# Expert stage of a hybrid block: every 64-token block in fp32, the first in straight code, further ones nested behind one branch

## The chip, the cores and the metric

The kernel runs on one core of one Trainium2 chip. The metric is the device time of one execution in microseconds (us), as the median of several runs. PE is the matrix engine (PEld its weight loads, PEq its sequencer), DVE the vector engine, ACT the scalar engine, POOL the GpSimd engine, and SP the engine that only issues transfers here.

## The reference, cut to what matters

The block computes an adaLN-modulated sub-layer of pooling heads and Mamba-2 heads with one output projection, then a mixture of experts, then a final RMSNorm. Only the expert part bears on the change:

```python
# 1024 tokens, D = 1024, 32 experts, two experts per token
# h: normed tokens; counts[e]: tokens of expert e (data dependent)
hu = h[rows_of_e] @ w13[e]                 # 1024 -> 2 x 512, fp32
a, b = split(hu)
y = (silu(a) * b) @ w2[e]                  # 512 -> 1024, fp32
out[rows_of_e] += g2 * gate * y
```

With the fixed inputs the 32 experts hold 2 to 397 tokens. In blocks of 64 tokens, 23 experts are one block, six are two (experts 8, 12, 17, 20, 26, 30), two are three (21, 22) and expert 16 is seven: 48 blocks.

## The kernel before, in words

Everything up to the routing is straight code. The expert stage then runs through the 32 experts in a Python loop, so each has its own instructions. The token counts are only known on the chip: each engine loads an expert's count into a register (`values_load`, L1194) and branches on it.

Weights. An expert needs twelve transfers of 512 KB (eight chunks of `w13`, four of `w2`). SP issues them in expert order (`load_to`, L793), at most `Q` = 4 in flight, into a ring of 39 slots; the ring's slots are tiles that earlier stages have given up (`raw`, `ybf`, `yps`, `wo`, `xc`, `g1b`, `h`, `x`, `sc`, `sh`), which is why the weight operands of one and the same matmul have many names in the rows. 36 transfers are issued ahead of the stage. Refills stand at the end of each expert: eight inside the branch (`refill()`), four behind the down projection.

Tokens. POOL gathers a block of token rows (`fetch`, L1067); PE transposes it (`transposed`, four matmuls named `px`, L1073), ACT copies it to `xa`. The results are weighed on DVE (L1145) and added to `acc` in memory by POOL's scatter (L1160).

Branches. `If(rv > 64, label e{e})` (L1264) has the code for more than 64 tokens as its fall-through, and the code for up to 64 tokens in its `Else`, so an expert of one block jumps.
- Up to 64 tokens: `up64` does the up projection in fp32, 64 matmul records on `xa`; `gated` (L1093, L1094) applies SiLU and the product; `turned` transposes the result (L1132) and, between its two halves, the next expert's tokens.
- More than 64: ACT and DVE split tokens and the eight `w13` chunks into fp16 high and low parts (L57, L59), and PE does three fp16 passes over 128 tokens (`up128s`); inside stands `If(rv > 128, label b{e})` (L1282), and below it `more` with branches L1221 and L1235 for still more tokens.
- Behind the If, for every expert: a hint, the down projection of the first 64 tokens (32 matmul records), the last four refills.

Hints. `aim(name)` puts a branch hint ("likely taken") for the named branch into every engine's instructions. `aim("e{e+1}")` stands ahead of the down projection of expert e, so on PE 32 matmul records ahead of the branch; `aim("b{e}")` stands first behind the fall-through of L1264.

Of the kernel before, what the change touches and what calls it, by code (L numbers as in the profile page):

```python
# [8 lines left out]
F32 = mybir.dt.float32  # L9
# [10 lines left out]
NT = 8  # L20
# [13 lines left out]
EARLY = 2  # L34
# [10 lines left out]
def block_kernel(ctx: ExitStack, tc: tile.TileContext, x, c, w_ada, b_ada, w_in, w_pool, pool_scale,  # L45
# [742 lines left out]
    lds = []  # L788

    def load_to(n):  # L790
        for i in range(loaded[0], min(n, 12 * NE)):
            e, k = divmod(i, 12)
            ld = SP.dma_start(ring[i % NR],  # L793
# [15 lines left out]
    for k in range(NWO, 8):  # L809
# [5 lines left out]
            + [sc2, sh2])  # L815
    spare = h2b[1:] + x2s[:1]
    NR = len(ring)
    G.dma_start(g1b, adad[0:1].to_broadcast([128, D]))
# [175 lines left out]
    with tc.manual_schedule(engines={mybir.EngineType.PE}):  # L994
        c_trans(0)
        for i in range(NT):
# [17 lines left out]
            if i < NT - 1:  # L1014
                c_h2(i)
            else:
                load_to(NR - 3)
# [31 lines left out]
    xa = pd1.tile([128, 8, 64], F32, name="xa")  # L1049
    xh = [pd1.tile([128, 8, 2, 64], F16, name=f"xh{i}") for i in range(2)]  # L1050
    wh = [t.bitcast(F16).rearrange("p (a n) -> p a n", a=2) for t in spare]
# [10 lines left out]

    def gather(e, b, r):
        some(r, b, fetch, xg0[e % 2] if b == 0 else xg1[e % 2] if b == 1 else xg2[b % 2], slots(b, e)[0])
# [11 lines left out]
    def prep(xg):  # L1076
        px = transposed(xg)
        A.activation(xa, px, AF.Copy)

    def parts(xg, a):  # L1080
        px = transposed(xg)
        split(xh[0][:, :, a, :], xh[1][:, :, a, :], px, HS)
# [5 lines left out]
    gT = [[vecs, onesf], [uinc, negm], [colv, pd1.tile([128, 128], F32, name="gt")]]  # L1088
# [9 lines left out]

    def up64(W, chunks_first):
        order = [(j, k) for k in range(8) for j in range(2)] if chunks_first else [(j, k) for j in range(2) for k in range(8)]  # L1100
        for j, k in order:
            for h in range(2):
                mm(p1s[j][64 * h:64 * h + 64, 0:256], xa[:, k, :], cols(W[k], 256 * h + 128 * j, 128), k == 0, k == 7)
            if k == 7:
                gated(j, 128)

    def up64s(P):
        for j in range(2):
            for k in range(8):
                for n, (a, b) in enumerate(PASS):  # L1110
                    for h in range(2):
                        mm(p1s[j][64 * h:64 * h + 64, 0:256], xh[a][:, k, 0, :], cols(P[k][:, b], 256 * h + 128 * j, 128),
                           k == 0 and n == 0, k == 7 and n == 2)
            gated(j, 128, INV)

    def up128s(P, step):
        for k0 in range(0, 8, step):
            ks = range(k0, k0 + step)
            js = (0, 1)
            order = [(n, k, j) for n in range(3) for k in ks for j in js]  # L1120
            if k0 + step == 8:
                order.sort(key=lambda t: t[2])
            for n, k, j in order:
                a, b = PASS[n]
                mm(p1s[j], xh[a][:, k].rearrange("p a t -> p (a t)"), cols(P[k][:, b], 256 * j, 256),
                   (n, k) == (0, 0), (n, k) == (2, 7))
                if k0 + step == 8 and (n, k) == order[-1][:2]:
                    gated(j, 256, INV)

    def turn(j, n, b0=0):  # L1130
        for i in range(n):
            PE.transpose(pgs[j][:, 128 * i:128 * i + 128], sils[j][:, 128 * i:128 * i + 128], identf)  # L1132
        if n == 1:
            A.activation(gT[b0][j], pgs[j][:, 0:128], AF.Copy)
        for a in (1, 0) if n == 2 else ():
            for i in range(2):
                A.activation(gT[b0 + a][i][:, 64 * j:64 * j + 64], pgs[j][:, 128 * i + 64 * a:128 * i + 64 * a + 64], AF.Copy)
# [9 lines left out]
    def turned(b, n, ahead=None, between=None):  # L1147
        turn(0, n, b)
        if ahead:
            prep(ahead)  # L1150
# [203 lines left out]
```

## Time and profile before

| what | us |
|---|---|
| three runs | 1222.46, 1227.43, 1234.52 |
| median | 1227.43 |
| the profiled execution, whole | 1233.29 |
| its span on the core | 1231.4 |
| PE busy in the span | 1018.3 |
| first matmul of the first expert | starts 534.11 |
| last matmul of the last expert | starts 1197.39 |

The profiled execution is one of its own, 4.0 us (span) above the median of the three. Its expert stage takes some 664 us, over half of the span; about 33 us lie behind it (reading `acc`, the final norm, the output). A timeline row gives a group of like instructions, its start, its length and, in brackets, how long the engine had been idle before it and what ended the wait; "issue" there means that nothing in the profile ended it but the engine's own instruction supply.

### The profile page before, as it was taken

How to read it: one execution, taken by the hardware profiler on the slowest of the kernel's cores; microseconds unless marked ns; L12 is line 12 of the kernel's file. 1: busy time of each engine (PE TensorE's matmuls, PEld its weight loads, DVE VectorE, ACT ScalarE, POOL GpSimd, SP SyncE). 2: the span in 40 equal slices, each digit the busy share in tenths (PEclk: the TensorE clock that was granted, in tenths of full speed). 3: DMA queues.
4: the chain of work that ended last, by engine and by line, in shares of the span. 5: the costliest groups of instructions: out<-in, count | busy, mean ns of one | idle time of the engine just before them, and what ended most of it. 6: DMA issues, size and time to landing. Idle time of an engine off the chain costs nothing.

```text
span 1231.4 us, 20504 instructions
## 1 busy us (share of the span) xinstructions
PE 1018.3 (83%) x7296; PEld 562.5 (46%) x7296; DVE 547.8 (44%) x1168; ACT 393.0 (32%) x747; POOL 253.3 (21%) x253
## 2 busy tenths in 40 slices
PE   4998988989898999667889787789888897797880
PEld 3433435666577555434444443434433343444440
DVE  6763669695788666710004041041413541040325
ACT  6434545465444322200114031041313431140312
POOL 1024324222220103311112121221122211211210
PEclk9998988999999999779989899899988999998995
DMA  9677773132201974789999999995789877999827
GB/s 315 198 193 189 222 226 79 37 80 44 60 1 53 373 283 148 291 275 365 356 355 355 361 374 360 368 367 187 231 272 365 310 233 217 340 369 366 307 31 281
DMA packets 115915, 302.82 MB, mean 246 GB/s; under 512 B 13556, under 2 KB 46506, under 8 KB 115602
## 3 DMA queue, kind: packets, MB, share of 16 engines
q1 hardware_dynamic: 96224, 259.83, 58.3%
q0 software_dynamic: 18160, 39.21, 13.9%
q8 instruction: 111, 1.82, 0.6%
q14 instruction: 202, 1.65, 0.4%
q10 hardware_dynamic: 1218, 0.31, 0.1%
HBM read 275.23 MB, written 24.07 MB: 243 GB/s over the span
## 4 chain that ended last, share of the span: by engine, by line
DMA 36%; PE 34%; issue 13%; DVE 10%; ACT 3%; POOL 2%; POOLq 1%; another core or an unknown queue 0%; DVEq 0%; SPq 0%; ACTq 0%
PE p L53 14%; DMA acc<-ye,idx 13%; DMA xg<-h2tab,idx 13%; PE proj L53 6%; PE po L53 5%; PE zp L53 3%; DMA abc<-acsd 2%; DMA table<-ent,dsti 1%; DMA wo<-in_w_dram 1%; DMA win<-in_w_ada_dram 1%; PE st L53 1%; PE pl L53 1%; DVE raw L1318 1%; DMA xt<-in_x_dram 1%; PE py L53 1%
## 5 line engine op out<-in xcount | busy, mean ns | idle before, releaser
L53 PE MATMUL proj<-hT,whl 128*128 128x512 f16 x768 | 182.9, 391 | 3.4 <-ACT hT L359 1.9
L1160 POOL DMA_INDIRECT acc<-ye,idx x48 | 74.1, 1543 | 238.9 <-DVE ye L1145 173.2
L53 PEld LDWEIGHTS <-whl 128*128 128x128 f16 x768 | 75.3, 100 | 103.4 <-issue 27.7
L1093 ACT ACTIVATE wp<-p 128x128 f32<-128x128 f32 (+1 forms) x37 | 11.4, 309 | 347.7 <-PE p L53 347.7
L1067 POOL DMA_INDIRECT xg<-h2tab,idx x48 | 51.4, 1070 | 312.9 <-PE p L53 176.5
L1145 DVE SCALAR_TENSOR_TENSOR ye<-p,gate,g2h 128x512 f32<-128x512 f32 x48 | 36.0, 750 | 175.1 <-PE p L53 145.2
L53 PE MATMUL p<-raw,xa 128*64 128x256 f32 x600 | 80.4, 421 | 28.3 <-issue 20.4
L53 PEld LDWEIGHTS <-xh 128*128 128x128 f16 (+1 forms) x816 | 66.7, 103 | 78.5 <-issue 10.5
L1094 DVE SCALAR_TENSOR_TENSOR wp<-p,wp 128x128 f32<-128x128 f32 (+1 forms) x37 | 12.3, 331 | 202.0 <-ACT wp L1093 195.3
L53 PEld LDWEIGHTS p<-raw,xa 128*64 128x64 f32 x600 | 54.9, 152 | 55.7 <-issue 42.0
L53 PE MATMUL zp<-wz,hT 128*128 128x192 f16 x768 | 69.3, 247 | 3.6 <-ACT zt L528 3.6
L53 PEld LDWEIGHTS <-hT 128*128 128x128 f16 x768 | 63.9, 99 | 6.4 <-issue 5.7
L53 PE MATMUL p<-wo,xa 128*64 128x256 f32 x368 | 50.9, 431 | 18.6 <-issue 15.7
L53 PE MATMUL po<-wo,yT 128*128 128x512 f16 x252 | 56.9, 379 | 0.0
L1094 DVE SCALAR_TENSOR_TENSOR wr<-p,wr 128x128 f32<-128x128 f32 (+1 forms) x37 | 12.3, 331 | 95.8 <-ACT wr L1093 92.7
L53 PEld LDWEIGHTS p<-wo,xa 128*64 128x64 f32 x368 | 33.4, 154 | 35.7 <-issue 26.5
L53 PE MATMUL p<-raw,xh 128*128 128x512 f16 (+1 forms) x234 | 48.8, 366 | 0.0
L1073 PE MATMUL px<-identf,xg 128*128 128x128 f32 x204 | 30.8, 278 | 14.5 <-DMA xg<-h2tab,idx 14.5
L1093 ACT ACTIVATE wr<-p 128x128 f32<-128x128 f32 (+1 forms) x37 | 11.4, 309 | 97.0 <-PE p L53 96.9
L593 POOL TENSOR_TENSOR abc<-acs,negm 128x768 f32<-128x768 f32 x16 | 24.7, 1606 | 77.6 <-DVE mh L635 77.5
L53 PEld LDWEIGHTS <-yT 128*128 128x128 f16 x252 | 24.7, 100 | 26.3
L53 PE MATMUL p<-yb,xa 128*64 128x256 f32 x224 | 30.6, 410 | 5.3 <-DMA raw<-in_w_dram 3.0
(483 smaller groups left out, 1887.2 us busy)
## 6 DMA issues: line engine op xcount, KB each, us to landing
raw<-in_w_dram SPq DMA_DIRECT2D x160, 512.0 KB
wo<-in_w_dram SPq DMA_DIRECT2D x80, 512.0 KB
yb<-in_w_dram SPq DMA_DIRECT2D x60, 512.0 KB
win<-in_w_ada_dram SPq DMA_DIRECT2D x32, 512.0 KB
yps<-in_w_dram SPq DMA_DIRECT2D x20, 512.0 KB
xc<-in_w_dram SPq DMA_DIRECT2D x19, 512.0 KB
xt<-in_w_ada_dram SPq DMA_DIRECT2D x16, 512.0 KB
win<-in_w_in_dram SPq DMA_DIRECT2D x16, 512.0 KB
```

Of the source, the lines that this page charges most:

```text
L53: return PE.matmul(o, l, r, start=start, stop=stop, skip_group_check=True)
L593: G.tensor_tensor(abc.rearrange("p c (r l) -> p c r l", r=3), acs[:, q2, hs, None].to_broadcast([128, 2, 3, 128]), negm[:, None, None, :]. ...
L1067: lastg[0] = G.indirect_dma_start(out=xg, out_offset=None, in_=h2tab, in_offset=bass.IndirectOffsetOnAxis(ap=ix, axis=0))
L1073: PE.transpose(pv[:, k], xg[:, k * 128:(k + 1) * 128], identf)
L1093: A.activation(sils[j][:, 0:n], p1s[j][:, 0:n], AF.Silu, scale=scale)
L1094: V.scalar_tensor_tensor(sils[j][:, 0:n], p1s[j][:, n:2 * n], scale, sils[j][:, 0:n], op0=ALU.mult, op1=ALU.mult)
L1145: V.scalar_tensor_tensor(y, p2, gt, g2h, op0=ALU.mult, op1=ALU.mult)
L1160: G.indirect_dma_start(out=acc, out_offset=bass.IndirectOffsetOnAxis(ap=ix, axis=0), in_=y, in_offset=None, compute_op=ALU.add)
L1318: V.scalar_tensor_tensor(js[i], ts[i], frs[:, i:i + 1], fnw, op0=ALU.mult, op1=ALU.mult)
```

## The change

All blocks are now computed in the fp32 form with 64 tokens. The loop body of an expert becomes: hint `aim("e{e}")` for its own branch, the gather two experts ahead, the weighing of the expert before, up and down projection of block 0 in straight code, and then `If(rv > 64)` whose fall-through holds the further blocks (`extra(1)`, which nests `extra(2)` and so on up to seven extra blocks, each level with a hint and an If of its own) and whose `Else` holds only the refills. So all twelve refills stand inside the If, in both its branches. The fp16 splits, `up64s`, `up128s`, `more` and the tiles `xh`, `wh` are gone; the two slots that the split used join the ring (41 slots; still 36 loads ahead of the stage). `xa` becomes three tiles: blocks 0 alternate between two, further blocks use the third.

```diff
-            + [sc2, sh2])
-    spare = h2b[1:] + x2s[:1]
+            + [sc2, sh2] + h2b[1:] + x2s[:1])
...
-                load_to(NR - 3)
+                load_to(NR - 5)
...
-    xa = pd1.tile([128, 8, 64], F32, name="xa")
+    xa = [pd1.tile([128, 8, 64], F32, name=f"xa{i}") for i in range(3)]
...
+    def up(W, i, chunks_first=False):
+        for j, k in [(j, k) for k in range(8) for j in range(2)] if chunks_first else [(j, k) for j in range(2) for k in range(8)]:
             for h in range(2):
+                mm(p1s[j][64 * h:64 * h + 64, 0:256], xa[i][:, k, :], cols(W[k], 256 * h + 128 * j, 128), k == 0, k == 7)
             if k == 7:
                 gated(j, 128)
...
+        def refill():
             loaded[0] = at_if
             lds.clear()
+            load_to(12 * e + 12 + NR)
...
+        def extra(b):
+            last = b == BLOCKS - 1
+            if not last:
+                aim(f"e{e}b{b + 1}")
+                if b == 1:
+                    maybe(e, 2)
+                maybe(e, b + 2)
+            if b == 1:
+                prep(rows(e, 1), 2)
+            up(W, 2)
+            g, p = gT[b % 2], p2s[1 + b % 2]
+            turned(g, None if last else lambda: prep(rows(e, b + 1), 2))
+            down(W, p, g)
+            put(b, p, ys[1 + b % 2])
+            if not last:
+                with tc.If(rv > 64 * (b + 1), preferred_fallthrough_block=True, label=f"e{e}b{b + 1}"):
+                    extra(b + 1)
...
+        aim(f"e{e}")
+        if e + 2 < NE:
+            gather(e + 2, 0, tokens(e + 2))
+        if e > 0:
+            weigh(p2s[0], slots(0, e - 1)[1], ys[3 * (e % 2)])
+            scatter_some(e - 1, 0, ys[3 * (e % 2)])
+        up(W, e % 2, e == 0)
+        turned(gT[0], (lambda: prep(xg0[(e + 1) % 2], (e + 1) % 2)) if e + 1 < NE else None)
+        down(W, p2s[0], gT[0])
         with tc.If(rv > 64, preferred_fallthrough_block=True, label=f"e{e}") as br:
...
+            extra(1)
+            refill()
         with br.Else():
-            fetch_ahead()
-            settle()
-            up64(W, e in (0,))
-            turned(0, 1, nxt)
             refill()
         lds.clear()
-        if e + 1 < NE:
-            aim(f"e{e + 1}")
-        down(W, p2s[0], 0)
-        load_to(12 * e + 12 + NR)
-        lds.clear()
```

On PE, before, the end of expert 2 and the branch of expert 3 stand as follows (`pg`, `px`: transposes; `p` with `vecs`, `onesf`: the down projection, its weights in slots that were `xc`, `g1b`, `h`; L1350 is the hint, L1194 the load of the count):

```order
L1132 MATMUL pg<-identf,wr 128x128
L1264 UNCONDITIONAL_BRANCH
L1171 UNCONDITIONAL_BRANCH
L1350 BRANCH_PREFETCH_HINT
L53 MATMUL p_5271<-xc_4045,vecs 32x512 x4
L53 MATMUL p_5271<-g1b,vecs 32x512 x4
L53 MATMUL p_5271<-xc_4046,onesf 32x512 x4
L53 MATMUL p_5271<-h_4047,onesf 32x512 x4
L1194 TENSOR_LOAD cnt
L1264 COMPARE_AND_BRANCH
```

The hint and the load of the count for the next branch stand between the end of the If and that branch, around the down projection. In the changed kernel PE comes to expert 2 (the end of expert 1's Else, then expert 2's own hint) like this:

```order
L1213 UNCONDITIONAL_BRANCH x2
L1270 BRANCH_PREFETCH_HINT
L1161 TENSOR_LOAD cnt
L53 MATMUL p_5267<-wo_3676,xa_5264 64x256 x2
L1139 UNCONDITIONAL_BRANCH
L53 MATMUL p_5267<-wo_3710,xa_5264 64x256 x2
```

Hint and count now stand right behind the place to which the jump of the expert before leads, ahead of the whole up projection. And this is the end of expert 2 and the beginning of its further blocks (`xa_5266` is the third `xa` tile):

```order
L53 MATMUL p_5270<-h_4047,onesf 32x512 x4
L1213 COMPARE_AND_BRANCH
L1270 BRANCH_PREFETCH_HINT
L1076 MATMUL px<-identf,xg_5260 128x2x2x32 x2
L1139 UNCONDITIONAL_BRANCH
L1076 MATMUL px<-identf,xg_5260 128x2x2x32 x2
L1139 UNCONDITIONAL_BRANCH
L53 MATMUL p_5267<-wo_3676,xa_5266 64x256 x2
```

The branch has moved from the head of an expert to its end, and an expert of one block jumps from here over the code of all its possible further blocks.

## Rows read from the trace of the kernel before

**Rows 1.** The page: engine totals, clock and DMA share by slice, the scatters.

```profile
PE 1018.3 (83%) x7296; PEld 562.5 (46%) x7296; DVE 547.8 (44%) x1168; ACT 393.0 (32%) x747; POOL 253.3 (21%) x253
...
PEclk9998988999999999779989899899988999998995
DMA  9677773132201974789999999995789877999827
...
L1160 POOL DMA_INDIRECT acc<-ye,idx x48 | 74.1, 1543 | 238.9 <-DVE ye L1145 173.2
```

**Rows 2.** PE's waits from 534 to 1200: total us, times, longest.

```profile
PE p L53 <- issue: 66.6, 32, 4.8
PE p L53 <- DMA raw<-in_w_dram: 9.0, 3, 3.1
PE p L53 <- DVE ye L1145: 7.8, 4, 4.0
PE p L53 <- ACT xh L57: 7.0, 9, 1.5
PE p L53 <- DVE xh L59: 5.9, 2, 3.4
```

**Rows 3.** PE's timeline, experts 0, 1, 2: start, length, work, idle before.

```profile
534.11 9.66 PE L53 MATMUL p<-raw,xa 128*64 128x256 f32 x64 [0.78 <-ACT xa L1078]
...
549.93 1.95 PE L53 MATMUL p<-raw,xa 128*64 128x256 f32 x16 [1.17 <-DVE ye L1145]
...
564.88 0.44 PE L53 MATMUL p<-wo,xa 128*64 128x256 f32 x2 [3.08 <-issue]
```

**Rows 4.** PE's timeline, expert 7 (one block) and the start of expert 8.

```profile
645.65 7.13 PE L53 MATMUL p<-raw,xa 128*64 128x256 f32 x64 [0.47 <-issue]
...
657.47 0.66 PE L1073 MATMUL px<-identf,xg 128*128 128x128 f32 x4
658.82 0.61 PE L53 MATMUL p<-h,xh 128*128 128x512 f16 x2 [0.69 <-ACT xh L57]
```

**Rows 5.** PE's timeline, experts 28 and 29 (one block each).

```profile
1133.40 8.69 PE L53 MATMUL p<-wo,xa 128*64 128x256 f32 x64 [2.88 <-issue]
...
1149.81 0.44 PE L53 MATMUL p<-x,xa 128*64 128x256 f32 x2 [3.06 <-issue]
```

**Rows 6.** Stretches: length, busy PE, PEld, DVE, ACT, POOL, granted clock, DMA share, GB/s.

```profile
645.60:652.70 7.10, 7.05 (x64) 5.41 (x64) 0.76 (x2) 0.28 (x1) 1.62 (x1) 1.00 1.00 362
683.40:693.60 10.20, 10.14 (x65) 6.61 (x66) 0.29 (x1) 0.30 (x2) 2.51 (x2) 0.70 1.03 387
1133.40:1142.10 8.70, 8.70 (x65) 5.74 (x66) 0.29 (x1) 0.28 (x1) 0.00 (x0) 0.82 1.03 366
```

**Rows 7.** Lines L1264, L1282, L1235, L1194 on PE's queue: ns min/median/max, first and last start.

```profile
L1264 PEldq COMPARE_BRANCH  x32: 74/4900/6967, 533.3 to 1182.2; - x32
L1282 PEldq COMPARE_BRANCH  x14: 74/350/6014, 670.4 to 1176.2; - x14
L1235 PEldq COMPARE_BRANCH  x3: 222/334/5544, 838.5 to 873.7; - x3
L1194 PEldq TENSOR_LOAD <-cnt x31: 302/308/352, 532.9 to 1160.5; - x31
```

**Rows 8.** PE's timeline behind b-branches: experts 8, 20, and 17 with its start.

```profile
672.59 1.06 PE L53 MATMUL p<-wo,uinc 128*32 128x512 f32 x8 [0.36 <-issue]
961.65 1.07 PE L53 MATMUL p<-yb,uinc 128*32 128x512 f32 x8 [0.36 <-issue]
879.52 2.61 PE L53 MATMUL p<-raw,vecs 128*32 128x512 f32 x16 [3.43 <-DVE xh L59]
903.89 1.38 PE L53 MATMUL p<-yb,uinc 128*32 128x512 f32 x8 [4.34 <-issue]
```

**Rows 9.** PE's timeline, end of expert 8 and start of expert 9.

```profile
675.52 1.92 PE L53 MATMUL p<-wo,vecs 128*32 128x512 f32 x16 [1.00 <-issue]
677.23 1.93 PE L53 MATMUL p<-wo,onesf 128*32 128x512 f32 x16
683.46 1.12 PE L53 MATMUL p<-wo,xa 128*64 128x256 f32 x4 [4.30 <-issue]
```

**Rows 10.** Weight queue (packets, MB, share) and all transfers, 534 to 840.

```profile
q1 hardware_dynamic: 27639, 100.67, 87.6%
534.00:840.00 306.00, 254.05 (x1843) 135.58 (x1843) 59.04 (x87) 59.16 (x142) 54.59 (x44) 0.92 1.01 362
```

**Rows 11.** PE's timeline: start of expert 16, and the stage's last matmuls.

```profile
804.72 0.66 PE L1073 MATMUL px<-identf,xg 128*128 128x128 f32 x4
1197.39 1.04 PE L53 MATMUL p<-xc,onesf 128*32 128x512 f32 x8
```

More of the change, by code (lines that the diff above doesn't have):

```diff
@@ L33 @@
 Q = 4
-EARLY = 2
+BLOCKS = 8
 YBF = {2: 2, 3: 3, 5: 4, 6: 5, 7: 6}
@@ L792, in load_to @@
             e, k = divmod(i, 12)
-            ld = SP.dma_start(ring[i % NR],
+            ld = SP.dma_start(lane[i],
                               w13[e, k * 128:(k + 1) * 128] if k < 8 else w2[e, (k - 8) * 128:(k - 7) * 128])
@@ L814, in block_kernel @@
     ring = (raw + [ybf[:, k * D:(k + 1) * D] for k in range(6)] + yps + wslots + xcb + [g1b] + h2b[:1] + x2s[1:]
-            + [sc2, sh2])
-    spare = h2b[1:] + x2s[:1]
+            + [sc2, sh2] + h2b[1:] + x2s[:1])
     NR = len(ring)
+    for i in range(12 * NE + 2 * NT + 1):
+        lane.append(ring[i % NR])
     G.dma_start(g1b, adad[0:1].to_broadcast([128, D]))
@@ L1061, in some, with rows @@
             f(x[0:64], ix[0:64])
+    def rows(e, b):
+        return (xg0[e % 2], xg1[e % 2])[b] if b < 2 else xg2[b % 2]
     def gather(e, b, r):
-        some(r, b, fetch, xg0[e % 2] if b == 0 else xg1[e % 2] if b == 1 else xg2[b % 2], slots(b, e)[0])
+        some(r, b, fetch, rows(e, b), slots(b, e)[0])
     def fetch(xg, ix):
@@ L1074, in transposed, with prep @@
         return px
-    def prep(xg):
+    def prep(xg, i):
         px = transposed(xg)
[L1078 to L1082, printed above, removed]
+        A.activation(xa[i], px, AF.Copy)
     p1s = [psd1.tile([128, 512], F32, name=f"p1{i}") for i in range(2)]
@@ L1145, in weigh, with turned, down @@
         V.scalar_tensor_tensor(y, p2, gt, g2h, op0=ALU.mult, op1=ALU.mult)
[L1147 to L1150, printed above, removed]
+    def turned(g, between=None):
+        turn(0, g)
         if between:
             between()
-        turn(1, n, b)
-    def down(W, p2, b, qs=(0, 2, 1, 3)):
-        for q in qs:
-            down_mm(p2, W, q, gT[b][q % 2][:, 64 * (q // 2):64 * (q // 2) + 64])
+        turn(1, g)
+    def down(W, p2, g):
+        for q in (0, 2, 1, 3):
+            down_mm(p2, W, q, g[q % 2][:, 64 * (q // 2):64 * (q // 2) + 64])
     def scatter(y, ix):
@@ L1184, in block_kernel @@
     lds.clear()
-    prep(xg0[0])
+    prep(xg0[0], 0)
     rvs[0] = nc.values_load(cnt[0:1, 0:1], min_val=0, max_val=T)
-    aim("e0")
     maybe(0, 1)
     for e in range(NE):
-        W = [ring[(12 * e + k) % NR] for k in range(12)]
-        P = wh + [t.bitcast(F16).rearrange("p (a n) -> p a n", a=2) for t in W[:6]]
+        W = lane[12 * e:12 * e + 12]
         rv = rvs.pop(e)
@@ L1301, in block_kernel @@
     man.__exit__(None, None, None)
-    fin = [ring[(12 * NE + n) % NR] for n in range(2 * NT + 1)]
+    fin = lane[12 * NE:]
     fnw, ts, js = fin[0], fin[1:NT + 1], fin[NT + 1:]
```

128 lines of the change are left out of this document (17 added, 111 removed).

## The prediction

> **What bounds the kernel now.** I began with the page [rows 1]. PE is busy 83% of the span, the matrix clock is mostly granted in full, and the DMA row stands at 9 or above through most of the second half, which is the expert stage. Two candidates, then: PE's chain or the weights. The stretch from 534 to 840 [rows 10] shows the transfers full (share 1.01, 362 GB/s), of which the weight queue moved 100.67 MB. An expert is 6.29 MB, so 16.0 experts came in 306 us, one per 19.1 us. With three experts loaded ahead, expert 16 is complete at about 534 + 14 x 19.1 = 801. PE begins it at 804.72 [rows 11]. So at expert 16 PE is level with the weights; behind it PE alone sets the pace, since expert 16 works for 80 us and the ring fills up.
>
> Next PE's waits [rows 2]. In the stage PE stood 66.6 us, in 32 waits, for nothing but its own instruction supply. That is more than all the waits for weights (9.0), the fp16 splits (7.0 and 5.9) and the weighing (7.8) together. The line that causes it is the branch [rows 7]: the compare at L1264 has a median of 4900 ns on PE's queue and a minimum of 74. The minimum is the fall-through, the median the jump. An expert of one block jumps. Expert 28 shows what is seen of it [rows 5]: PE's array stands idle 2.88 us before it and 3.06 us behind it, the rest of the 4.9 us lying under matmuls still in the array.
>
> [...]
>
> **What one block costs.** Expert 7 from its first matmul to the first of expert 8 [rows 4] is 657.47 - 645.65 = 11.82 us: up, transposes, down, no gap. The changed kernel does 48 of these (the 48 scatters of [rows 1]): 48 x 11.82 = 567.4 us.
>
> A first further block must have its tokens transposed and copied: in the old form 658.82 - 657.47 = 1.35 us [rows 4], and the changed kernel has the same four transposes and a copy by ACT. Nine experts: 9 x 1.35 = 12.2. Later blocks have this under `turned`, so nothing.
>
> The first expert ran cold: 549.93 - 534.11 = 15.82 [rows 3], less 11.82 and less the gap of 1.17, is 2.8 us. It stays.
>
> Losing the fp16 form costs and brings next to nothing for two blocks. Expert 8 with its exit took 683.46 - 657.47 = 26.0 us in the old form [rows 4, 9]; in the new one 2 x 11.82 + 1.35 + 1.2 (exit, below) = 26.2.
>
> **What an exit costs: the term that decides.** There are 31 exits, 22 from experts of one block and 9 from larger ones. Consecutive one-block experts of before start 14.95 us apart at the first pair [rows 3] (564.88 - 549.93) and 16.41 at the last, experts 28 and 29 [rows 5]; over the 15 such pairs the mean is 16.18, so an exit with its slow clock costs 16.18 - 11.82 = 4.4 us. The change adds to it: the load of the count, 308 ns [rows 7], lay under the down projection and now stands behind the landing, ahead of the up projection. So an exit whose jump stalls costs 4.7 us.
>
> An exit whose jump doesn't stall costs at least 0.36 (a jump that went well [rows 8]) + 0.31 for the count = 0.67 us, and in the changed program's Else PE's queue also waits for its own last matmuls. From above it is bounded by 1.17, the shortest gap at a stage's start [rows 3]. I take the upper bound, 1.2.
>
> Which of the two applies hangs on the hint. Before, it stood 32 matmul records ahead of the branch, and the jump stalled nearly always. Now the whole up projection lies between, some 12 us. That a long lead can help, the b-branches show: hint at the beginning of the fp16 form, branch some 15 us on, and the gap behind it was 0.36 us at experts 8 and 20 [rows 8], and in five of six in all (the median of L1282 is 350 ns [rows 7]). What speaks against it is the sixth. Expert 17 had the same lead, and its jump cost 4.34 us [rows 8]. What differs is what came just before: expert 16 had left by a stalled jump (the longest of L1235, [rows 7]) just ahead of 879.52, and the hint stands behind the one down projection that began there. Expert 9's hint too stood right behind a jump, at the end of expert 8's Else, ahead of the down projection that began at 675.52 and with more time than usual to its branch; its gap is the longest of its kind, 4.30 us [rows 9]. A hint right behind a landing thus had no effect in the places that I can find. In the changed kernel every `aim("e{e}")` stands right behind the landing of the expert before: the order shows the end of the Else, the hint, the count. So I expect the hint to be lost as a rule, and the state to keep itself up, as a stalled landing is followed by a lost hint and so by the next stall.
>
> [...]
>
> I count 20 stalled exits and 2 good ones, the share of before (of its short gaps at one-block experts, 1.17 and 0.47 stand in [rows 3, 4]): 20 x 4.7 + 2 x 1.2 = 96.4. The nine larger exits have their hint behind a fall-through, as the b-branches had, and then a short jump over the Else: 9 x 1.2 = 10.8.
>
> **Sum.** 567.4 + 12.2 + 2.8 + 96.4 + 10.8 = 689.6 us for PE's stage. Before it was 1197.39 + 1.04 - 534.11 = 664.3 [rows 3, 11]. So +25.3 us. What lies ahead and behind is unchanged. On the profiled span of 1231.4 this is 1256.7; that execution is 4.0 above the median, so on the median 1227.4 it is 1252.7, say 1253.
>
> **What I cost at nothing, and its cover.** The refills: SP now passes its own branch with four loads in flight instead of up to eight, and all slots of a larger expert come free only at its end. By the sum PE reaches expert 16 at 534 + 18 x 11.82 + 2.7 + 2.8 + 2.4 + 14 x 4.7 = 821, the weights at 801: 20 us of cover. Behind expert 16, 29 slots hold experts 17 and 18 and five chunks of 19; 17 and 18 take over 42 us, the seven missing chunks some 11 at 19.1 / 12 = 1.6 each. If the first cover is gone, as in the next case, the loads set expert 16. The two more slots are worth two chunks, 3 us of lead that PE can't use. The fp16 splits gone from ACT and DVE free engines that the end does not wait for, but for the 5.9 us of [rows 2], which the sum already leaves out.
>
> **Rivals.**
> The hint works (ends on the other side): with up to 12 us of lead the target is there at every branch, L1213 jumps in 0.36 us, and all 31 exits cost 1.2. PE alone would need 619.6 us; but expert 16's last weights come at 801, so its first block ends at about 804. From there 29 blocks (342.8), seven first further blocks (9.5) and 15 exits (18.0) end at 1174: 24 us sooner, about 1203. It speaks for it that five of six long leads worked; against it, that those five stood behind a fall-through. It decides from a mean exit of (664.3 - 567.4 - 12.2 - 2.8 - 10.8) / 22 = 3.2 us downward: below it the change is faster. Chance 0.21.
>
> Half the hints work: behind expert 16 four of eight one-block exits stall, 4 x 3.5 = 14 us more than in the case above, so PE ends near 1188 and the time is near 1217; with a third working, near 1222. Chance 0.14, nearly all of it within 1%.
>
> More stalls than I count: the short jump over the Else behind a larger expert stalls too. Its nearest row is the jump of 1.00 us at expert 8 [rows 9], the farthest the 4.34 of [rows 8]. If half of nine pay 3.5 us more, +16: about 1269. Chance 0.07.
>
> My forecast, 1253, has 0.58, with a range of its own from 1243 (exits of 4.2) to 1263 (all 22 stalled).
>
> **Numbers.** A difference under 1% is about what cannot be told from none here. Slower: 0.58 + 0.07 less 0.02 for stalls that are shorter than I think = 0.63. Faster: 0.21 + 0.02 of the half case = 0.23. Within 1%: 0.14. To hold 8 in 10 the range must take in much of the working hint below and some of the extra stalls above: 1201 to 1267.
>
> **What would show it.** In the changed kernel's profile the compare at L1213 on PE's queue should again have a median near 4900 ns, and one-block experts should start some 16.5 us apart with about 3.4 us idle before each, labelled issue. Up projections behind them should take 8.7 us. No wait for weights should end a PE gap from expert 1 to 15. If instead the compare's median is near 350 ns and up projections take 7.1 us throughout, the hint works, and the weights should appear as PE's releaser ahead of expert 16. If the stage starts later than 534, the change touched what I took as untouched.

## The result and the profile after

The changed kernel takes 1276.18 us in the median (four runs, 1274.92 to 1278.36), the kernel before on the same chips 1230.05. The ratio is 1.038, with a 95% interval from 1.032 to 1.044: slower, as forecast, but by 46 us instead of 25, and outside the range. The profiled execution has a span of 1276.6 us. Ratios here and below leave out executions that were more than 1.5% above the fastest of their kernel; of the variants this concerns one execution, of blocks4_ahead.

In what follows an exit is the way from an expert's branch to the next expert. It is short when the jump's record on PE's queue is some 0.35 us, and stalled when it is several us.

PE's waits in the expert stage are the first thing to read. This is that view of the changed kernel from 530 to 1250 (what waited, for what: total us, times, longest):

```profile
PE px L1076 <- DMA xg<-h2tab,idx: 45.4, 10, 14.6
PE p L53 <- PEq L1213: 15.9, 5, 3.8
PE p L53 <- DVE ye L1115: 10.8, 13, 0.9
PE p L53 <- DVEq L1189: 10.5, 9, 1.3
PE p L53 <- DMA raw<-in_w_dram: 8.7, 3, 3.2
PE px L1076 <- issue: 8.0, 1, 8.0
```

The 66.6 us of "issue" of [rows 2] are gone as such; what a stalled jump costs now stands mostly under PEq and in the lines for weights, a short exit under "DVE ye" (0.83 us each). New, and the largest, is the first row: the transposes of the next tokens wait for the gather. One of its ten is the first expert's (14.6, before too); the other nine are 30.8 us, and the 8.0 in the last row is the same wait at expert 16. That makes 38.8 us which no term of the sum had. They cost more than their length, since the clock falls behind them as it does behind a stall (0.81 over expert 11's up projection, behind a gap of 3.27 us): expert 24, with 2.9 us of them, takes 13.3 us outside its gaps, expert 23, which has none, 11.8 (mean granted clock 0.91 and 1.00).

The branch itself, line L1213 on PE's queue (ns min/median/max), against [rows 7]:

```profile
L1213 PEldq COMPARE_BRANCH  x40: 74/342/6005, 547.1 to 1233.8; - x40
```

The median fell from 4900 ns to 342, but the 40 records hold the larger experts' fall-throughs and short jumps too, so the jumps have to be counted one by one. Nine of the 22 one-block exits that another expert follows stall (of experts 0, 2, 4, 6, 10, 14, 18, 24, 28), 13 are short. PE's timeline shows both at experts 9, 10 and 11:

```profile
683.09 2.81 PE L53 MATMUL p<-wo,xa 128*64 128x256 f32 x24 [1.08 <-DVEq L1189]
...
695.73 0.65 PE L53 MATMUL p<-sh,xa 128*64 128x256 f32 x4 [0.83 <-DVE ye L1115]
...
710.78 4.93 PE L53 MATMUL p<-raw,xa 128*64 128x256 f32 x28 [3.27 <-PEq L1213]
```

Expert 9 with a short exit lasts 12.64 us, expert 10 with a stalled one 15.05. Expert 9 entered without a slow clock (1.00 from 683.1 to 690.3), so a short exit is 12.64 - 11.82 = 0.8 us (taken as 1.2). The nine stalled ones leave PE idle for 2.3 to 3.8 us, 3.1 in the mean.

Where the time went, by parts of the span, worked out from PE's timeline (first up or transposing matmul of experts 0, 16 and 17, end of the last matmul):

| part, us | before | by the prediction | after |
|---|---|---|---|
| up to expert 0's first matmul | 534.1 | 534.1 | 535.5 |
| experts 0 to 15 | 270.6 | 287 | 270.3 |
| expert 16 (seven blocks) | 80.1 | 85.3 | 95.2 |
| experts 17 to 31 | 313.7 | 317 | 335.6 |
| behind PE's last matmul | 32.9 | 32.9 | 40.1 |
| span | 1231.4 | 1256.7 | 1276.6 |

The 287 take all 14 one-block exits of the first half as stalled, as the prediction's paragraph on cover does. The first half came out 17 us better than that and no worse than before; everything from expert 16 on came out 28 us worse, and the tail 7.

**What makes the gathers late.** POOL's timeline of the changed kernel around one of these waits, with PE's row under it:

```profile
695.76 0.95 POOL L1070 DMA_INDIRECT xg<-h2tab,idx  x1 [11.22 <-PEq L1213]
697.68 1.57 POOL L1128 DMA_INDIRECT acc<-ye,idx  x1 [0.98 <-issue]
712.76 1.01 POOL L1070 DMA_INDIRECT xg<-h2tab,idx  x1 [13.51 <-PE p L53]
714.44 1.58 POOL L1128 DMA_INDIRECT acc<-ye,idx  x1 [0.66 <-issue]
730.01 1.02 POOL L1070 DMA_INDIRECT xg<-h2tab,idx  x1 [13.99 <-PEq L1213]
```

```profile
723.23 0.63 PE L1076 MATMUL px<-identf,xg 128*128 128x128 f32 x4 [3.37 <-DMA xg<-h2tab,idx]
```

POOL's gathers stand 17 us apart here, in one-block experts, more than the 12.6 to 15 us of PE. The gather of 712.76 is the one that PE waits for until 723.23. The engine named as POOL's releaser had long been done; what POOL does in between stands in its waits at the line of the If, here of before, then of after, and at the line of the nested Ifs of after (ns min/median/max):

```profile
L1264 POOLq EVENT_SEMAPHORE  x69: 17/43/43, 536.4 to 1190.6; - x69
```

```profile
L1213 POOLq EVENT_SEMAPHORE  x115: 17/43/10703, 537.2 to 1240.3; - x115
```

```profile
L1189 POOLq EVENT_SEMAPHORE  x42: 17/43/10268, 683.7 to 1230.8; - x42
```

These waits belong to the Else, which therefore holds more than the refills: in these programs a path that skips transfers brings their semaphores to where the other path leaves them, and waits first until what was issued on them has landed. In before the records of each Else but the first and the last name six of POOL's eight transfer semaphores, not the two just used, and none of the 69 waits lasts over 43 ns. The nested blocks of the change put up to seven scatters and as many gathers into one If, so the records of every Else name all eight, the two just used included. So POOL issues the scatter of the expert before and then stands until it has landed: 10.7 us in expert 10's Else, 72 us over the stage as the sum of these records, and 33 us more at L1189. The sums are too low, as POOL also stands idle ahead of some of the short records: from its branch to the last of these waits it needs 8.7 us in the median of the 23 Elses. Only then does it come to the next expert's gather.

POOL waited for scatters before, too, but elsewhere:

```profile
L1160 POOLq EVENT_SEMAPHORE  x104: 17/43/7077, 549.8 to 1195.5; - x104
```

These add up to 58.5 us, and the eleven over 0.5 us all stand at larger experts, in front of a scatter. New are the waits in one-block experts, in front of a gather.

The same wait explains the tail. POOL's last scatters before (two rows) and after (two rows):

```profile
1190.63 1.55 POOL L1160 DMA_INDIRECT acc<-ye,idx  x1 [7.62 <-issue]
1199.53 1.55 POOL L1160 DMA_INDIRECT acc<-ye,idx  x1 [7.35 <-DVE ye L1145]
```

```profile
1235.38 1.56 POOL L1128 DMA_INDIRECT acc<-ye,idx  x1 [8.98 <-issue]
1244.27 1.56 POOL L1128 DMA_INDIRECT acc<-ye,idx  x1 [7.33 <-issue]
```

Before, the last scatter is issued 1.1 us behind PE's end (1198.4), now 7.8 us behind it (1236.5), since expert 30's scatter of 1235.38 must land first.

### The profile page after: what moved, and what is told of

Read it like the earlier page. It is cut to its first block, busy times and chain, and to the rows that moved or that the text cites. A ratio compares the mean times of both kernels' runs of the same rounds, so it can differ in the third digit from the quotient of the medians.

```text
span 1276.6 us, 21711 instructions
## 1 busy us (share of the span) xinstructions
PE 1058.3 (83%) x8104; PEld 614.9 (48%) x8104; DVE 449.5 (35%) x1090; ACT 322.3 (25%) x650; POOL 249.0 (20%) x253
## 3 DMA queue, kind: packets, MB, share of 16 engines
q8 instruction: 98, 1.61, 0.5%
## 4 chain that ended last, share of the span: by engine, by line
DMA 50%; PE 21%; issue 11%; DVE 9%; ACT 3%; POOLq 3%; POOL 2%; another core or an unknown queue 2%; DVEq 0%; SPq 0%; ACTq 0%
DMA acc<-ye,idx 21%; DMA xg<-h2tab,idx 21%; PE proj L53 6%; PE po L53 5%; PE zp L53 3%; DMA abc<-acsd 3%; PE p L53 2%; POOLq L1055 1%; DMA table<-ent,dsti 1%; PE st L53 1%; PE pl L53 1%; DMA win<-in_w_ada_dram 1%; DVE wo L1238 1%; DMA adad<-adr 1%
## 5 line engine op out<-in xcount | busy, mean ns | idle before, releaser
L53 PE MATMUL p<-raw,xa 128*64 128x256 f32 x1064 | 130.3, 396 | 23.6 <-PEq L1213 6.4
L53 PEld LDWEIGHTS p<-raw,xa 128*64 128x64 f32 x1064 | 89.7, 143 | 65.3 <-issue 36.6
L1093 DVE SCALAR_TENSOR_TENSOR wp<-p,wp 128x128 f32<-128x128 f32 x48 | 14.0, 292 | 278.8 <-ACT wp L1092 214.0
L1092 ACT ACTIVATE wp<-p 128x128 f32<-128x128 f32 x48 | 13.3, 278 | 379.3 <-PE p L53 355.8
L53 PE MATMUL p<-wo,xa 128*64 128x256 f32 x712 | 89.1, 390 | 9.1 <-DVE ye L1115 3.4
L53 PEld LDWEIGHTS p<-wo,xa 128*64 128x64 f32 x712 | 58.2, 140 | 39.0 <-issue 18.1
L1093 DVE SCALAR_TENSOR_TENSOR wr<-p,wr 128x128 f32<-128x128 f32 x48 | 14.0, 292 | 148.8 <-ACT wr L1092 148.6
L53 PE MATMUL p<-yb,xa 128*64 128x256 f32 x400 | 52.8, 397 | 13.4 <-DMA raw<-in_w_dram 5.5
L1081 ACT ACTIVATE xa<-px 128x512 f32<-128x512 f32 x57 | 34.1, 598 | 103.2 <-PE px L1076 83.8
L1076 PEld LDWEIGHTS px<-identf,xg 128*128 128x128 f32 x228 | 27.2, 148 | 63.4 <-issue 62.7
L1092 ACT ACTIVATE wr<-p 128x128 f32<-128x128 f32 x48 | 13.3, 278 | 149.5 <-PE p L53 149.5
L53 PEld LDWEIGHTS p<-yb,xa 128*64 128x64 f32 x400 | 34.7, 143 | 29.9 <-issue 18.0
```

The costliest lines, as they stand in the source:

```text
L53: return PE.matmul(o, l, r, start=start, stop=stop, skip_group_check=True)
L1076: PE.transpose(pv[:, k], xg[:, k * 128:(k + 1) * 128], identf)
L1081: A.activation(xa[i], px, AF.Copy)
L1092: A.activation(sils[j][:, 0:n], p1s[j][:, 0:n], AF.Silu, scale=scale)
L1093: V.scalar_tensor_tensor(sils[j][:, 0:n], p1s[j][:, n:2 * n], scale, sils[j][:, 0:n], op0=ALU.mult, op1=ALU.mult)
```

## The experiments

Two theories went into them. POOL: the late gathers are the cause, through POOL's waits in the Else. EXIT: it is PE's stalled jumps, and late gathers fill time that is lost anyway. Ratios are to the kernel before, run beside each variant.

### POOL's waits

**settle_behind** moves weighing and scatter ahead of the gather on POOL:

```diff
-        if e > 0:
-            weigh(p2s[0], slots(0, e - 1)[1], ys[3 * (e % 2)])
-            scatter_some(e - 1, 0, ys[3 * (e % 2)])
...
         lds.clear()
+        weigh(p2s[0], slots(0, e)[1], ys[3 * ((e + 1) % 2)])
+        scatter_some(e, 0, ys[3 * ((e + 1) % 2)])
```

> The changed kernel with one edit: the weighing and scatter of an expert's first block stand right behind its own If, no longer in the next expert's body behind the gather two experts ahead. Theory POOL (POOL is late because at the end of each Else it waits for its own scatter, issued just before, to land; so the gathers come late and PE's transposes of the next tokens wait 30.7 us in nine places and 8.0 us in a tenth): the scatter is issued some 5 us sooner against that wait and the gather waits all but vanish, 25 to 38 us less, 1238 to 1251. Theory EXIT (the excess lies in PE's stalled jumps; the late gathers only fill time that PE would lose anyway): within 8 us of the changed kernel, 1268 to 1284.

1264.8 us, ratio 1.029 (1.022 to 1.036): 11 less. The records of the waits in the Else fell from 72 to 56 us only, since now the gather's own landing is waited for, and PE's waits for gathers are 30.0 us in nine and 1.9 at expert 16, where they were 30.8 and 8.0. Neither theory's number; it shows that the order of the two transfers matters less than that both are waited for.

**xg3** gathers three experts ahead:

```diff
-        if e + 2 < NE:
-            gather(e + 2, 0, tokens(e + 2))
+        if e + 3 < NE:
+            gather(e + 3, 0, tokens(e + 3))
```

> The changed kernel with a third token buffer for first blocks, so that POOL gathers three experts ahead instead of two; the buffer takes one ring slot (40 instead of 41). Theory POOL: a gather that lands up to one expert late is still in time, PE's 39 us of waits for the next tokens vanish, 25 to 39 us less than the changed kernel, 1237 to 1251, unless POOL's own pace per expert is slower than PE's; then POOL falls further behind and the waits only shrink by a third to a half, 1256 to 1264. Theory EXIT: within 8 us.

1272.2 us, ratio 1.037 (1.028 to 1.047). PE's waits for tokens are as long as ever:

```profile
PE px L1077 <- issue: 22.9, 4, 13.5
PE p L53 <- PEq L1214: 22.2, 7, 4.4
PE px L1077 <- DMA xg<-h2tab,idx: 15.8, 3, 7.4
```

22.9 + 15.8 = 38.7 us: the wait only moved to later experts. So it is not one transfer's latency, it is POOL's pace per expert.

**blocks4** leaves the order alone and takes the number of transfers in the If down (later blocks run in the run-time loop):

```diff
-BLOCKS = 8
+BLOCKS = 4
...
-                maybe(e, b + 2)
+                if b + 2 < BLOCKS:
+                    maybe(e, b + 2)
```

> The changed kernel with four blocks in nested code instead of eight (later blocks in the run-time loop that stood behind the eighth; only expert 16 uses it, for three blocks), and no gather beyond the fourth. The transfers skipped by a one-block expert then use seven of POOL's eight transfer semaphores instead of all eight, so that POOL's Else no longer waits for the lane of every transfer just issued. Theory POOL: its waits in the Else (72 us) fall by half or more, PE's waits for tokens with them, 15 to 35 us less outside expert 16; the loop adds some 20 us at expert 16. Theory EXIT: nothing but the loop, 10 to 30 us more.

1282.0 us, ratio 1.048 (1.038 to 1.058), slower as a whole, and yet the clearest run, as the loop's price stands by itself. The records of each Else now name seven of the eight semaphores, not the one of the scatter just issued. Its waits on PE, then POOL's waits in the Else and at the scatter:

```profile
PE px L1076 <- DMA xg<-h2tab,lix: 33.8, 3, 14.5
...
PE px L1076 <- DMA xg<-h2tab,idx: 4.0, 1, 4.0
```

```profile
L1214 POOLq EVENT_SEMAPHORE  x92: 17/43/4800, 532.6 to 1241.9; - x92
L1128 POOLq EVENT_SEMAPHORE  x111: 17/43/7748, 542.0 to 1246.1; - x111
```

The first row is the loop's own gather (index `lix`) at expert 16. Elsewhere the waits for gathers fell from 38.8 us to 4.0 and the records of POOL's waits in the Else from 72 to 15 (from the branch to the last wait 2.9 us in the median, where it was 8.7). At the scatter's line they rose from 6 to 39 us, as in before mostly at larger experts: POOL still waits, but seldom ahead of a gather that PE needs next. By parts (table below) it loses 43 us at expert 16 and gains 10 before it, 17 behind it and 7.6 in the tail: 34 us, at the upper end of what POOL expected. The exits are not the reason, as ten of them stall here and nine did. The edit also makes each expert's code shorter and gives POOL more time at expert 16; neither was separated, but the gain before expert 16 and in the tail can't come from the second.

**blocks4_ahead** issues the loop's gather one block ahead.

> The kernel blocks4 with the run-time loop's gather issued one block ahead (the first ahead of the loop, the next behind the transposes of the present one). In blocks4 the loop's three rounds lose 34 us waiting for their gathers, all at expert 16. Theory POOL: what is left is the stage without late gathers and without the late last scatter: 25 to 40 us less than blocks4, 1242 to 1257, that is 20 to 35 us under the changed kernel. Theory EXIT: the time comes back to the changed kernel's, 1265 to 1280.

1297.2 us (1287.0 to 1309.7), ratio 1.049 (1.036 to 1.061): no gain; expert 16 still took 134.6 us (137.8 in blocks4). The loop's rounds wait for more than their gather. The trace shows a part of what for, at the loop's line:

```profile
L1196 POOLq DRAIN  x4: 47/2429/7991, 875.7 to 907.8; - x4
```

At the end of a round the engines wait for each other. The longest of these records starts at 875.73, right behind POOL's issue of the round's scatter, and ends at 883.72; PE's next round starts at 884.86, after 10.3 us of idle time. So a round, too, stands behind a scatter that was just issued.

### The place of the hint

**no_hint** is the changed kernel without `aim(f"e{e}")`.

> The changed kernel without the hints for the experts' own branches (the hints of the further blocks stay). Theory EXIT: all 22 exits of one-block experts stall, 13 more than now, each worth 2.3 us of gap and, as an expert behind a stalled one is slow already, up to 1.5 us of clock: 30 to 50 us more, 1305 to 1325. Theory POOL: PE's longer exits give POOL time, the waits for tokens shrink instead, 0 to 25 us more, 1276 to 1300.

1303.4 us, ratio 1.063 (1.053 to 1.073). The branch:

```profile
L1212 PEldq COMPARE_BRANCH  x40: 70/4648/7424, 544.4 to 1262.5; - x40
```

All one-block exits stall, and PE's waits for gathers shrink to 9.7 + 4.4 us. It lies between the two expectations: the hint as it stands is worth 27 us, 30 by the ratios.

**hint_mid** was to move the hint to the middle of the up projection.

> The changed kernel with one edit: the hint for an expert's own branch stands in the middle of the up projection (ahead of its second half), no longer right behind the landing of the expert before; the lead falls from about 12 us to about 8. Theory EXIT: the nine stalled jumps of one-block experts become jumps of 0.35 us, each worth about 2.3 us of gap and 1.5 us of slower clock: 30 to 40 us less, 1236 to 1246. Theory POOL: the jumps become short too, but POOL's pace holds the stage, and PE's gaps come back as longer waits for gathers: 0 to 15 us less. If the place of the hint does not matter: the jumps still stall at every second one-block expert, no change.

1275.6 us, ratio 1.038 (1.031 to 1.045). The built program explains it: a hint comes out at the beginning of its basic block, and the up projection starts none, so on PE nothing moved. With settle_behind's edit as well, **settle_hint** is settle_behind again on PE:

> Both edits at once: scatter right behind the If, hint in the middle of the up projection. Theory POOL with the exits as second cause: the gains add until the weights of expert 16 (complete at about 801) set the pace, 55 to 70 us less than the changed kernel, 1206 to 1221. Theory EXIT alone: as hint_mid, 1236 to 1246.

1263.9 us, ratio 1.028 (1.022 to 1.035).

**hint_block** gives the hint a block of its own, ahead of the last quarter of the up projection; **hint_twice** does so and keeps the first one:

```diff
+            if hint and (j, k) == (1, 4):
+                with tc.block():
+                    aim(hint)
```

> The changed kernel with the hint moved for real: in hint_mid the hint came out at the beginning of its basic block, where it was before; here a block of its own holds it, three quarters through the up projection, about 6 us of matmuls ahead of the branch. Theory EXIT: the nine stalled jumps become jumps of 0.35 us, 30 us less, 1240 to 1250. Theory POOL: the jumps become short, but the time stays within 12 us, as the waits for gathers grow by what the exits lose. If the place does not matter: every second jump stalls as before.

> The changed kernel with the hint for an expert's own branch given twice: right behind the landing, as it is, and again three quarters through the up projection. In the runs so far a hint was followed by a short jump (0.35 us) nearly always when the jump before had stalled, and by a stalled one when the jump before had been short, wherever the hint stood. If a hint is lost because of something that the first hint clears, the second one works: all exits short, 20 to 30 us less if POOL keeps step, 5 to 15 us less if POOL's pace holds PE (theory POOL), 1262 to 1272. If not, jumps alternate as before and the time stays within 5 us.

1271.2 us, ratio 1.039 (1.028 to 1.050), and 1273.8 us, 1.033 (1.025 to 1.040). Neither made the stalled jumps short; in hint_block 13 of 22 stall. In hint_twice, as in the changed kernel, settle_behind and hint_mid, the even one-block experts stall (3.7 us and more) and the odd ones do not (at most 1.3). This holds behind larger experts too: 18 stalls, while 9, 13, 23 and 27 do not, though all five come behind a larger expert that left by a short jump. That speaks against the jump before as the cause and points to the place in the code: counted in the built program, an expert is 1919 instructions on PE. In the trace of the changed kernel instructions come in packets of one size on queue q8: 98 of them, 1.61 MB together, 16.4 KB each. The author assumed that the code lies in instruction blocks of one length, that the place of hint and branch in their blocks counts, and that two experts nearly fill a whole number of blocks, so that the odd ones lie alike and the even ones too. The length of a block is shown by no run.

**align_hit** and **align_miss** test that with code that never runs. It brings an expert from 1919 to 2048 instructions, a length chosen by that assumption:

```diff
                 with tc.If(rv > 64 * BLOCKS, preferred_fallthrough_block=False):
+                    for _ in range(65 if e else 0):    # align_miss: 65 for every expert
+                        PE.transpose(pgs[0][:, 0:128], sils[0][:, 0:128], identf)
```

> The changed kernel with 65 dummy transposes on PE in code that only an expert of more than 512 tokens would run, so never here, for every expert but the first. [...] Theory PLACE (where hint and branch lie in their blocks decides, not what came before): from expert 1 on all lie as the odd ones did, and all jumps are short but expert 0's. Theory HISTORY (a hint behind a short jump is lost): short and stalled go on alternating. Time by PLACE: if POOL's pace holds PE, 5 to 15 us less than the changed kernel, 1261 to 1271; if not, 25 to 35 less. By HISTORY: within 5 us.

> The same with the dummies in the first expert too, so that all experts lie as the even ones did. Theory PLACE: all 22 jumps of one-block experts stall although the hints are there, and the time is that of no_hint, 1295 to 1308. Theory HISTORY: as the changed kernel, 1270 to 1282.

1266.7 us, ratio 1.028 (1.022 to 1.034), and 1288.6 us, ratio 1.049 (1.043 to 1.055). PE's branch line and two of PE's waits, of align_hit and then of align_miss:

```profile
L1215 PEldq COMPARE_BRANCH  x40: 74/340/4787, 543.2 to 1224.2; - x40
```

```profile
PE px L1076 <- DMA xg<-h2tab,idx: 38.0, 13, 4.9
```

```profile
L1215 PEldq COMPARE_BRANCH  x40: 74/3798/6265, 546.9 to 1235.6; - x40
```

```profile
PE p L53 <- PEq L1215: 44.9, 14, 4.4
PE px L1076 <- DMA xg<-h2tab,idx: 15.1, 5, 5.5
```

In align_hit every one-block jump from expert 1 on takes 0.34 to 0.62 us; in align_miss all 22 stall, with the same code run and the hint in the same place in it. PLACE holds without an exception as to which jumps are short; whether the hint, the branch or the target has to lie right was not separated, and the blocks themselves were not shown. The times are just as telling: 22 us between all short and all stalled, where the stalls alone are over 40. When exits are short PE waits more for POOL (38.0 and another 5.4), when they are long less (15.1 and 5.2). One expectation was off: align_miss was to equal no_hint and is 15 us faster. Its jumps, the last expert's counted, took 3.0 to 6.3 us, those of no_hint 4.0 to 7.4, so a hint in the wrong place seems to shorten the stall.

### Both causes together

**settle_align** is settle_behind with align_hit's dummies, **blocks4_ahead_twice** is blocks4_ahead with the second hint, **blocks4_align** is blocks4 with dummies (35 and 101) that put every branch where align_hit has it.

> align_hit and settle_behind together. Theory PLACE with POOL as the second bound: short jumps everywhere and the late scatters of settle_behind gone; about 10 us each below the changed kernel, 1250 to 1260, POOL's waits in the Else holding the rest. If exits were the larger part: 1225 to 1240. HISTORY: as settle_behind, 1258 to 1270.

> Both of the two edits above: four nested blocks with the loop's gather ahead, and the hint twice. If the second hint makes the exits short, nothing holds them back here: 10 stalled exits at about 3.5 us less, 1210 to 1225, under the kernel before. If hints alternate as before: as blocks4_ahead within 5 us.

> blocks4 with dummy transposes in never-run code (35 for the first expert, 101 for each other), so that every expert's code is 1280 instructions on PE and every branch from expert 1 on lies as in align_hit. Both causes are then away: POOL's waits on all its transfer semaphores, and the stalled jumps. The run-time loop at expert 16 stays and costs what it cost in blocks4 (137.8 us for that expert against 95.2 in the changed kernel). Theory POOL plus PLACE: blocks4's stalled jumps vanish, each worth some 3.5 us, 25 to 38 us less than blocks4, 1244 to 1257; with the loop's 43 us taken off that would be 1201 to 1214. If something else holds PE: waits for tokens come back as in align_hit, 1265 to 1280.

settle_align: 1264.9 us, ratio 1.026 (1.020 to 1.033), no better than settle_behind: with short exits PE's waits for gathers rose to 45.7 us. blocks4_ahead_twice: 1276.5 us, 1.037 (1.028 to 1.045); ten of its exits stall, partly at other experts than in blocks4_ahead, and the second hint did not make them short. blocks4_align: 1279.9 us, 1.038 (1.033 to 1.043), far from the 1244 to 1257 expected though all jumps but the first are short. By parts, each from the profiled execution (that of align_miss, 1279.6 us, is its fastest, 9 us under its median):

| us | experts 0 to 15 | expert 16 | 17 to 31 | tail |
|---|---|---|---|---|
| before | 270.6 | 80.1 | 313.7 | 32.9 |
| after | 270.3 | 95.2 | 335.6 | 40.1 |
| no_hint | 305.2 | 90.7 | 335.7 | 37.8 |
| align_miss | 273.2 | 93.7 | 336.0 | 39.5 |
| align_hit | 261.6 | 94.0 | 338.9 | 39.7 |
| blocks4 | 260.2 | 137.8 | 318.9 | 32.6 |
| blocks4_align | 254.4 | 150.0 | 306.9 | 32.8 |
| before_align2 | 263.0 | 80.9 | 298.0 | 32.7 |

Behind expert 16 the four kernels with waits on all eight semaphores take 336 to 339 us whatever their exits do; blocks4 takes 17 us less, and with short exits another 12 less. That is the answer to POOL against EXIT: behind expert 16 short exits gain nothing while POOL needs its 8 to 9 us in each Else (its median is 8.4 to 8.8 in all four), and only with POOL out of the way do they count. In no_hint the stalls fill that time and PE waits only 8.7 us for gathers there, so the two limits lie close together. In the first half the exits count, until the weights stop it: in blocks4_align PE comes to expert 16 at 790.87, before its weights.

```profile
792.20 0.65 PE L53 MATMUL p<-wo,xa 128*64 128x256 f32 x4 [0.69 <-DMA wo<-in_w_dram]
793.49 1.12 PE L53 MATMUL p<-wo,xa 128*64 128x256 f32 x4 [0.63 <-DMA wo<-in_w_dram]
...
798.87 1.12 PE L53 MATMUL p<-xc,xa 128*64 128x256 f32 x4 [1.40 <-DMA xc<-in_w_dram]
```

Its first block takes 24 us there instead of 14, so the 6 us won by then and 4 more are given back at expert 16; the stage as a whole is 5.6 us shorter than that of blocks4, and it began 5.8 us later.

### The kernel before with better hints

**before_hint** and **before_twice** put hints for the next expert at the beginning of the one-block path (in before_hint written into the middle, from where it comes out at the beginning; in before_twice again three quarters through, and the old one stays). **before_align** is before_hint with never-run dummies (six transposes for every expert but the first, 103 for that), meant to put every branch where the short jumps of before_hint (experts 5, 6, 7 and 28) had it; **before_align2** moves the branches by another 28 instructions and gives two-block experts the hint in the Else of the b-branch. The edit of before_align, cut to the one-block path and without its dummies:

```diff
         with br.Else():
             fetch_ahead()
             settle()
+            if nh:
+                aim(nh)            # nh: the next expert's label
             up64(W, e in (0,))
...
-        if e + 1 < NE:
-            aim(f"e{e + 1}")
         down(W, p2s[0], 0)
```

> The kernel before with one edit: the hint for the next expert's branch stands in the middle of the up projection (one block) or ahead of the transposes of the gated values (more), no longer ahead of the down projection: a lead of about 6 us instead of 1.5. If lead is what was missing: the jumps at L1264 fall from 4.9 us to 0.35, 15 to 30 us less than the kernel before, 1200 to 1215, held by the weights up to expert 16. If a hint is lost for another reason: within 8 us of before.

> The kernel before with two more hints for the next expert's branch in the one-block path: at its beginning and three quarters through the up projection; the old one ahead of the down projection stays. If more hints shorten the jumps at L1264: 15 to 28 us less than before, 1202 to 1215, held by the weights until expert 16. If the hints alternate: half of that, 1215 to 1225. If they are lost as before: within 5 us of before.

> [...] Theory PLACE: nearly all jumps at one-block experts become short; PE is then level with the weights until expert 16, and the time falls by 15 to 30 us against the kernel before, 1200 to 1215. Theory HISTORY: as before_hint, 1215 to 1226.

> before_align with every branch L1264 moved 28 instructions to the front within its block (89 dummies for the first expert instead of 103), towards the middle of the places at which jumps were short in before_hint and before_align, and with the next expert's hint for two-block experts at the beginning of the Else of the b-branch instead of at their beginning. Theory PLACE: before_align had 9 short jumps of 22; if the new place is nearer the middle, 14 or more, and 3 to 12 us less than before_align, 1205 to 1214. If the place is wrong: fewer short jumps and 1217 to 1230.

1220.8 us, ratio 0.995 (0.991 to 0.999); 1224.5 us, 0.992 (0.988 to 0.996); 1216.8 us, 0.989 (0.985 to 0.994); and **1209.1 us, 0.982 (0.977 to 0.986)**, 1.8% under the kernel before. The branch line of before_align2:

```profile
L1267 PEldq COMPARE_BRANCH  x32: 68/3156/6284, 533.0 to 1161.2; - x32
```

Its time is in the expected span, but not for the expected reason: 5 of 22 jumps are short, in before_align 9. The records of the line add up to 80 us, in before to 113, in before_align to 70. Behind expert 16 the stage takes 298.0 us instead of 313.7. That the hints gave the gain over before fits these sums but is not shown by them, since the dummies move code as well; why before_align2 is ahead of before_align is open, and the place that makes every jump short was not found for this kernel.

## Why the prediction was right and wrong

- **The bound: right for before. The direction: right by luck.** PE's chain, level with the weights up to expert 16, then PE alone: so it was in before. But the sum forecast "slower" through 20 stalled exits. With the nine that did stall its own terms give 689.6 - 11 x 3.5 = 651 us, 13 less than before: the change would have been faster. It was slower through a cost that the sum did not have. That "no wait for weights should end a PE gap from expert 1 to 15" can't be held against the profile, as gaps behind stalled jumps carry a weight's name there.
- **A block costs 11.82 us: right.** In expert 16 PE's compares between nested blocks stand 11.7 us apart (849.97, 861.70, 873.42). The first further block's wait is 0.69 us as expected, the nine larger exits 1.1 to 1.3 us of idle time (1.2 taken).
- **The exit: wrong in count, about right in price.** Predicted 20 stalled of 22 at 4.7 us; measured nine, at 2.3 to 3.8 us of idle time and 1.5 to 1.7 us of slower clock in the next expert where nothing else disturbs it (7, 19, 25, 29). The slower clock in that price stands in the rows of before: an up projection of 7.13 us at a granted clock of 1.00 behind 0.47 us of idle time, of 8.69 us at 0.82 behind 2.88 us [rows 4 to 6]. In the first half 8 of 14 exits are short, worth some 28 us at 3.5 each, of which waits for gathers take 10.6 back and the slow clock behind them more; 17 are left. The two "good" exits of before were no short jumps either: behind the gaps of 1.17 and 0.47 us stand records of 3.3 and 2.6 us on PE's queue. The step that failed is "a hint right behind a landing had no effect": in align_hit every hint stands right behind a landing, and from expert 1 on every one-block jump takes 0.34 to 0.62 us. What experts 9 and 17 of before had in common was taken for a cause from two cases; the runs show the place in the code instead. The rival "half the hints work" had the count about right (13 of 22), through another cause, and its 1217 us would need POOL out of the way.
- **All 22 stalled, the upper end of the forecast's own range (1263): not in the changed kernel.** 13 are short there. All 22 stall in no_hint (median of the line 4648 ns, 1303.4 us) and in align_miss (3798 ns, 1288.6 us).
- **"What I cost at nothing": here the forecast broke.** The paragraph gave the cover for SP's refills and for the splits, and the sum took what lies behind PE's end as unchanged. Neither followed POOL past the new branch, with the transfers that the Else has to account for: a term put at nothing without a reason. It is 38.8 us of PE waiting for gathers, the slow clock behind them, and 7.2 us in the tail. In the first half 10.6 of the 38.8 are outweighed by exits that cost less than forecast; 8.0 stand in expert 16 and 20.2 behind it. blocks4 takes nearly all of it away and gains 34 us outside expert 16.
- **Sum.** Forecast 25 us, measured 45 by the spans: first half -17, expert 16 +10, behind it +19, tail +7, start +1.4 against the forecast, together +20.

## What to carry to other kernels

When code moves into a branch, count for each engine that issues transfers what the other path must now wait for: here a skipped transfer cost its engine a wait on that semaphore, and the nested blocks made it a wait for everything in flight (up to 10.7 us of POOL in one Else). Where two engines take turns to set the pace, making one faster can show nothing, as here short exits did on top of settle_behind (1264.9 us against 1264.8); take the stage apart and look at the stretch in which the other one is out of the way. A branch hint can be lost through where the code lies (here the one-block jumps from expert 1 on were all short or all stalled, 22 us apart), so before a kernel is ranked by it, run it once with never-run code put in ahead of it.

## What the runs showed of the hardware

- A taken jump on PE over an expert's further code took 4.0 to 7.4 us without a hint (no_hint), 0.34 to 0.62 with one that works (align_hit), 3.0 to 6.3 with one that does not (align_miss); a fall-through 0.07.
- Whether a hint works was decided by 130 instructions that never ran: the same executed code had its one-block jumps from expert 1 on all short (align_hit) or all stalled (align_miss), 22 us apart.
- A scatter of 64 rows was waited for up to 10.7 us, from 714.93 in the changed kernel, while the transfers were full (share 1.00 from 714.4 to 725.7); in before and in blocks4 up to 7.1 and 7.7 us.
- Behind a wait of 3.3 us the granted clock was 0.81 over the next up projection, which took 8.7 us instead of 7.2 (experts 11 and 9 of the changed kernel).
